# Thresholded attention on one core: GpSimd's queue held in the order of a written table, the second quad loaded by pairs, and another table

## The chip, the core and the metric

The kernel runs on one core of one Trainium2 chip. The metric is the device time of one execution in microseconds; lower is better. A core has five engines with a queue each: TensorE (PE in the profile, with its weight loads as PEld), VectorE (DVE), ScalarE (ACT), GpSimd (POOL) and SyncE (SP, which here only issues transfers). Transfers run on 16 DMA engines.

## The reference

Q, K and V are random float32 arrays of 8 batches, 12 heads, 512 positions and 64 dimensions; the threshold is 0.1.

```python
scores = einsum('bhqd,bhkd->bhqk', Q, K) * scale          # scale = 1/8
weights = exp(scores - max(scores)); weights /= sum(weights) + 1e-10
weights = where(weights > threshold, weights, 0)
weights /= sum(weights) + 1e-10
out = einsum('bhqk,bhkd->bhqd', weights, V)
```

On such data hardly a row has a weight above 0.1, so nearly the whole output is zero. The few rows that are not zero have one key each that passes.

## The kernel before, in words

The 96 heads are 48 pairs, the pairs are 24 quads (a quad is two pairs, four heads), and eight pairs are a group; there are six groups. The kernel does not compute the attention of every row. It writes zeros over the whole output, finds by rough tests the rows in which a weight may pass the threshold, and computes those rows exactly, at most 16 for each pair; a slow loop at the end takes over if there were more than that.

**For each quad**, the main part does these steps (names as in the table, function names with `do_` before them):

- `k`, `q` (lines 394 to 404, issued by SP): loads of K, four transfers of 128 KB, and of Q, one of 512 KB. K goes into a ring of four buffers, Q into one of three.
- `qcast` (GpSimd, line 411): Q to float16, one instruction for each pair.
- `ktr`, `qtr` (PE, lines 421 and 432): transposes of K and Q into PSUM.
- `kev`, `qev` (ACT or DVE, lines 387 and 389): copies of these from PSUM, two halves each.
- `kh` (GpSimd, line 391): the float32 keys to float16.
- `bits` (DVE, line 457) and `size` (PE, line 503): the norms of the rows, by a trick on the bits.
- `sc` (PE, line 467), `ex` (ACT, line 475, or DVE, line 477), `g` (PE, line 496): for each pair and each 128 keys the scores, their exponentials, and sums and sums of a high power over the keys, collected in one PSUM bank (`acc`) for the whole group. There are 384 exponentials of 128x512; ACT computes them by its table, DVE by shifting bits.
- `z` (SP, line 626): a write of 512 KB of zeros to the output.

**For each group**, a chain of small steps follows: `evac`, `test`, `flags`, `rank`, `key`, `oh`, `idx`, `idxev`, `base` find the rows to be computed; `gather` (GpSimd, line 556) fetches their Q by an indirect transfer, `split`, `xtr`, `xev`, `xqk`, `xexp`, `xcut`, `xkeep` compute their scores against all keys and find the key that passes; `xvi`, `xoi` make indices; `gv` (GpSimd, line 612) fetches the row of V by an indirect transfer, and `scatter` (GpSimd, line 619) writes it into the output by a third one. A scatter waits for its `gv` and for the zero writes of its group. The next group's sums wait for `evac`, since there is one `acc` bank.

**What sets the order.** All these steps are entered in a plan as numbered operations, and a long string, `ORDER`, lists them one by one: the number, the engine (A, D, G, P, S) and the buffers to take. `Plan.run` walks the string and traces each operation on the engine that it names. The framework then schedules what was traced by its own rules. To hold the written order, each instruction is wrapped in `keep`:

```python
keep = tc.keep_in_program_order
```

It ties an instruction to the instruction traced just before it on the same engine, and the framework may not swap those two. An indirect transfer is traced as two instructions on GpSimd, a register move (which the framework adds, without `keep`) and the transfer itself; `affine_select`, by which constants are made, has such a move too. No other operation of the table has one.

The string is found outside the kernel, by a search over a model of the engines. The numbers in it follow the order in which operations are entered: 12 constants first, then for each unit of loading its steps, after each fourth quad the 21 steps of its group, at the end five others. A unit is what is loaded and prepared together: a quad, but for quad 0, whose two pairs are two units.

Read out of the string, the order on SP and on GpSimd before is this (k, q, z and the casts with the number of their quad, a and b for its pairs where these are apart; gather, gv, split and scatter with their group):

```
SP:     k0a k0b q0b k1 q1 k2 q2 z0 k3 k4 q3 z1 z2 q4 k5 k6 q5 q6 z3 z4 q7 k7 q8 q9 z5 q10
        k8 k9 k10 k11 k12 q11 z6 z7 z8 z9 q12 k13 z10 k14 k15 q13 z11 q14 z12 q15 k16 q16 k17
        z13 q17 z14 q18 q19 k18 z15 q20 k19 z16 q21 k20 z17 q22 k21 q23 k22 z18 k23 z19 ... z23
GpSimd: tri test_a lane slot_no row_no key_i test_b qcast0a key_no test_w qcast0b kh0b
        qcast1 kh1 qcast2 kh2 kh3 qcast3 kh4 qcast4 kh5 qcast5 kh6 qcast6 gather0 qcast7 kh7
        split0 qcast8 qcast9 qcast10 gv0 kh8 kh9 scatter0 gather1 qcast11 kh10 split1 kh11
        qcast12 gv1 kh12 qcast13 kh13 scatter1 qcast14 kh14 qcast15 gather2 qcast16 kh15 split2
        qcast17 kh16 qcast18 gv2 kh17 qcast19 kh18 qcast20 scatter2 gather3 split3 qcast21 kh19
        qcast22 kh20 gv3 kh21 qcast23 kh22 scatter3 kh23 gather4 split4 gv4 gather5 split5
        scatter4 gv5 scatter5
```

(q0a is issued by ACT in both.)

Of the kernel before, what the change touches and what calls it, by code (L numbers as in the profile page):

```python
# [18 lines left out]
104S 114D 93A 97P1.6.12 96D 92A 87P 98D 99A 115P3.4.11 149P0.5 145S 95A 117D 118P1.6.10 150A6 100P 120D 151A
101P 119D 209S1 121P2.4.9 152G0 124P0.6.8 116D 123A 129P1.5.7 131A 122D 132P3.4.6 130A 127P 249S2 134D 126A  # L20
211P2.5 143D0 125A 135P1.4.5 148G0 212A5 213D 144P 128P 137A 136D 138P0.6.4 214G3 133A 153P2.5 140D 290S1 154A
141P 155D 139D 156P1.4.3 159P3.6.2 157A 162P2.5.1 158D 142P 161A 163D 165P0.1.0 164A 170P4.6.13 250S0 184D2 160A
210G1 173P2.5.12 171D 172A 185P 168P 175A 167D 291S2 176P3.4.11 174A 215P5.6 166D 177A 179P1.2.10 216D 169P 181A
217D 182P 180D 186S 252P0.3 178D 218P5.6.9 253D4 254A 221P1.2.8 183P 222A 248S 223D 255G2 224P3.4.7 220A 293P0.1
187D1 226A 227P2.6.6 219A 225D 332S1 188P4 229A 189D 230P 246D1 251G0 228A 190P 294A3 232P3.5.5 295D 235P2.6.4
331S0 233A 231P 234D 296G1 237A 247P 191D 256P0.1 236D 238P3.5.3 257A 241P4.6.2 292G1 192D1 244P 242A 243D 193P2
258A 394S0 239A 297P0.4 194D2 259P1.6.1 287D0 298A 196G1 261D 240A 288P 435S2 262P0.3.0 260A 195D 299D 245P 263A
264D 265P5.6.13 268P1.2.12 328D2 267A 273P0.4.11 333G0 271P 289S 275A 270D 329P 269A 276P3.6.10 266D 279P2.4.9
274A 277D 282P1.5.8 281A 476S1 272P 280D 283A 334P0.3 278A 284D 300P1.2.7 335A2 303P4.6.6 336D 393S3 285P 305A
301D 337G0 286P 302A 304D 306P0.5.5 309P3.6.4 307A 314P1.2.3 308D 197G1 312P 395G1 311A 316D 317P0.4.2 315A  # L30
434S2 320P5.6.1 318D 319A 198P2 321D 199A1 323P0.1.0 338P2.4 325A 324D 200P5 436G0 339A 322D 340A 310D 475S1
369D1 400P0.1 201A1 341P2.6.13 477G1 344P3.4.12 342D 313P 346A 326P 343D 345A 327P 202D 516S0 203D 370P 353P
347P2.5.11 205D 204D 396P3.4 349A 348D 206G2 397D1 398A 350P5.6.10 351A 352D 355P2.4.9 578S3 399G3 356A
358P3.5.8 357D 354P 360A 359D 361P2.6.7 364P4.5.6 363A 401D 367P 402D 362A 366D 437P0.3 517S0 365A 403P1.6.5
431D0 406P2.5.4 438A0 368P 407D 405A 330S 409P0.4.3 404A 372D0 412P2.6.2 410A 414D 373P1 413A 371S 432P 374D
411A 441P0.6 439D 375P 408A 417P2.4.1 376D 440G2 420P1.3.0 433S 418A 377D0 415P 422A 421D 416P 207G 419A 378P5
442A 443D 474S 423P2.3.13 379D1 426P1.4.12 380D 424D 425A 478P0.6 381G0 427A 429P 428D 579S2 479A9 444P3.5.11
472D2 518G0 447P1.2.10 480A 450P0.4.9 445D 448A 430P 473P 619S2 449A 446D 481G1 453P1.6.8 451A 452D 458P2.3.7
454A 456P 455D 459A 461P0.5.6 464P1.4.5 460D 463A 457P 466A 462D 467P2.6.4 515S 482P3.5 468A 469D 470P 483A 484D
519P0.4 465D 660S1 485P2.6.3 382G0 523P3.5 520D8 521A 383P1 471P 487A 486D 522G0 384A0 488P0.4.2 513D1 491P1.6.1  # L40
489A 385P2 580G1 493D 490A 701S0 492A 524D 525A 514P 554D0 497P 386A0 494P0.4.0 581P3.6 387D 496A 388D 620S1
499P1.5.13 582A7 555P 389D 502P2.4.12 500D 583A 391G1 495A 390D 505P3.6.11 556S 501D 504A 508P0.1.10 506D 584G3
503A 498P 510D 509A 526P4.5.9 529P2.3.8 661S0 528A 527D 511P 530A 532P0.1.7 507D 535P4.5.6 531A 533D 540P2.6.5
537A 618S 512P 542D 536A 538P 541A 534D 585P0.3 543P4.5.4 702S2 586A 587D 546P2.6.3 539P 545D 544A 621G0
549P1.3.2 616D2 547A 622P0.5 550A 551D 763S3 552P 548A 623D6 588P2.4.1 624A 591P1.3.0 553P 590D 589A 625G2
594P0.6.13 593D 592A 663P4.5 595A 557D1 597P1.2.12 392G 764S1 596A 602P0.3.11 664D5 665A 600P 662G1 617P 599A
603D 558P6 598A 605P4.5.10 804S2 559D 608P0.2.9 607A 606D 560P 666G1 601P 610A 561D 609D 604A 611P1.5.8 626P4.6
562D1 612A 667P0.2 703G0 614P 627A 628D 668D 659S 563P3 669A 657D1 613A 629P1.6.7 632P0.4.6 564D0 630D 631A 658P
# [784 lines left out]
```

## Time and profile before

| | |
|---|---|
| median of 3 runs | 193.63 us (192.74 to 194.64) |
| the profiled execution's own time | 194.19 us |
| its span, first to last instruction | 192.4 us |
| busy: PE, DVE, ACT, GpSimd | 170.1, 164.3, 146.7, 86.2 us |
| mean granted clock of PE | 0.955 |
| moved by DMA | 38.44 MB, 200 GB/s over the span |

In the rows of the profile an instruction stands as output<-input by tile names; L411 is line 411 of the kernel. A group's row ends with busy time, mean duration in ns, and the idle time of the engine ahead of these instructions with what ended it. The two rows of slices cut the span into 40 parts of 4.8 us; a digit is the busy share in tenths. In GpSimd's timeline the bracket holds the idle time before an instruction and the instruction that released it; a queue entry such as "POOLq MOVE" is one of the sequencer and not counted as busy.

### The profile page before, as it was taken

To read this page: it belongs to the slowest core of one execution; us is meant where nothing else is said; L and a number is where in the kernel's file an instruction comes from. 1 tells how busy PE (TensorE), PEld (TensorE's weight loads), DVE (VectorE), ACT (ScalarE), POOL (GpSimd) and SP (SyncE) were. 2 spreads that over 40 slices of the span, in tenths; PEclk is the share of its full clock that TensorE was granted. 3 is DMA by queue.
4 is the path that set the end of the run, shared out by engine and by line. 5 is a ranking of instruction groups with operands and counts; after the bars stand their busy time and mean duration, and the time that the engine had idled before them with its cause. 6 is when DMAs were issued, how large, how long until landed. Compare 5 with 4: busy or idle time off the path is not lost.

```text
span 192.4 us, 5896 instructions
## 1 busy us (share of the span) xinstructions
PE 170.1 (88%) x2272; PEld 69.7 (36%) x2272; DVE 164.3 (85%) x343; ACT 146.7 (76%) x295; POOL 86.2 (45%) x129
## 2 busy tenths in 40 slices
PE   7699969999998698999999999989999999997910
PEld 2343332443333143433453434433433533334300
DVE  7699978999999599999999999899799999996040
ACT  2679867799976588899999979979799898951010
POOL 7744243286552427255564534770442723103322
PEclk9889997999999889999999999999999999999975
DMA  5997898898988799989999996969895000000000
GB/s 135 257 269 213 200 376 191 253 363 203 347 173 189 169 354 345 227 200 319 300 266 326 282 291 197 282 184 235 226 382 202 1 3 0 10 0 5 8 2 8
DMA packets 67439, 38.44 MB, mean 200 GB/s; under 512 B 51882, under 2 KB 64240, under 8 KB 67408
## 3 DMA queue, kind: packets, MB, share of 16 engines
q1 hardware_dynamic: 66560, 37.50, 68.3%
q0 software_dynamic: 576, 0.27, 0.8%
q8 instruction: 19, 0.31, 0.7%
q10 hardware_dynamic: 272, 0.26, 0.5%
q14 instruction: 12, 0.10, 0.2%
HBM read 25.56 MB, written 12.78 MB: 199 GB/s over the span
## 4 chain that ended last, share of the span: by engine, by line
PE 40%; DVE 29%; DMA 11%; issue 9%; POOL 6%; SPq 2%; ACT 1%; POOLq 0%; DVEq 0%; ACTq 0%
DVE e L477 16%; PE bank L467 15%; PE acc L496 13%; DVE v L457 5%; DMA k<-in_K_dram 5%; PE bank L582 4%; PE bank L421 3%; DMA q<-in_Q_dram 3%; POOL qh L411 3%; DVE kt L389 2%; DMA vr<-in_V_dram,idx 2%; PE acc L503 2%; DVE qk L389 2%; PE bank L432 2%; POOL qk L391 2%
## 5 line engine op out<-in xcount | busy, mean ns | idle before, releaser
L475 ACT ACTIVATE e<-bank 128x512 f16<-128x512 f32 x226 | 118.5, 613 | 11.9 <-PE bank L467 11.0
L477 DVE TENSOR_SCALAR e<-bank 128x512 int16<-128x512 f32 x158 | 101.3, 682 | 4.7 <-PE bank L467 4.2
L467 PE MATMUL bank<-qk 64*128 64x512 f16 x384 | 67.6, 390 | 5.5 <-POOL qk L391 1.9
L496 PE MATMUL acc<-e,w_sum 128*32 128x512 f16 x384 | 57.7, 393 | 0.3 <-ACT e L475 0.2
L496 PE MATMUL acc<-e,w_pow 128*32 128x512 bf16 x384 | 57.4, 393 | 0.0
L411 POOL TENSOR_SCALAR qh<-q 128x512 f16<-128x512 f32 x48 | 34.1, 710 | 21.9 <-DMA q<-in_Q_dram 7.8
L391 POOL CAST qk<-kt 128x1024 f16<-128x1024 f32 (+1 forms) x24 | 24.8, 1036 | 27.0 <-ACT kt L387 12.4
L467 PEld LDWEIGHTS <-qk 64*128 64x128 f16 x384 | 18.3, 95 | 43.2 <-issue 35.8
L496 PEld LDWEIGHTS <-w_sum 128*32 128x32 f16 x384 | 13.9, 96 | 25.6 <-issue 20.0
L387 ACT COPY kt<-bank 128x512 f32<-128x512 f32 (+1 forms) x30 | 17.1, 588 | 7.6 <-PE bank L421 6.9
L457 DVE TENSOR_SCALAR v<-qk 128x1024 int32<-128x1024 int32 x24 | 19.0, 795 | 2.7 <-POOL qk L391 1.9
L421 PE MATMUL bank<-identity_f,k 64*128 64x64 f32 x384 | 17.5, 228 | 1.4 <-DMA k<-in_K_dram 1.3
L421 PEld LDWEIGHTS bank<-identity_f,k 64*128 64x128 f32 x384 | 15.5, 141 | 6.7 <-issue 2.6
L612 POOL DMA_INDIRECT vr<-in_V_dram,idx x6 | 6.5, 1084 | 22.1 <-DVE keys L528 9.7
L389 DVE COPY kt<-bank 128x512 f32<-128x512 f32 (+1 forms) x20 | 13.0, 659 | 1.5 <-PE bank L421 0.8
L496 PEld LDWEIGHTS <-w_pow 128*32 128x32 bf16 x384 | 13.6, 96 | 0.2
L619 POOL DMA_INDIRECT out_dram<-vr,idx x6 | 6.3, 1044 | 16.1 <-DVE e L477 4.7
L389 DVE COPY qk<-bank 128x512 f16<-128x512 f16 (+1 forms) x30 | 11.7, 411 | 1.8 <-PE bank L432 1.4
L387 ACT COPY qk<-bank 128x512 f16<-128x512 f16 (+1 forms) x20 | 10.9, 566 | 2.2 <-PE bank L432 2.2
L432 PE MATMUL bank<-identity_h,qh 64*128 64x64 f16 x384 | 10.5, 192 | 2.0 <-POOL qh L411 1.8
L432 PEld LDWEIGHTS <-qh 64*128 64x128 f16 x384 | 8.8, 96 | 9.1 <-POOL qh L411 4.6
L582 PE MATMUL bank<-kt,xq 128*32 128x512 f32 x96 | 11.6, 597 | 0.4 <-ACT xq L387 0.4
(95 smaller groups left out, 103.7 us busy)
## 6 DMA issues: line engine op xcount, KB each, us to landing
k<-in_K_dram SPq DMA_DIRECT2D x96, 128.0 KB
out_dram<-zero SPq DMA_DIRECT2D x24, 512.0 KB
q<-in_Q_dram SPq DMA_DIRECT2D x23, 512.0 KB
q<-in_Q_dram ACTq DMA_DIRECT2D x1, 256.0 KB
q<-in_Q_dram SPq DMA_DIRECT2D x1, 256.0 KB
qs<-in_Q_dram,idx POOLq DMA_INDIRECT x6, 4.4
vr<-in_V_dram,idx POOLq DMA_INDIRECT x6, 4.3
out_dram<-vr,idx POOLq DMA_INDIRECT x6, 2.5
```

The costliest lines, as they stand in the source:

```text
L387: keep(nc.scalar.copy(dst, src))
L389: keep(nc.vector.tensor_copy(dst, src))
L391: keep(nc.gpsimd.tensor_copy(dst, src))
L411: keep(nc.gpsimd.tensor_scalar(dst, src, ALPHA, 1.0, op0=ALU.mult, op1=ALU.mult))
L421: keep(nc.tensor.matmul(bank_at(("kp", u), i)[:, c:c + D], lhsT=src[ps, n0 + n, r, :], rhs=identity_f32[ps, ps], is_transpose=True, start= ...
L432: keep(nc.tensor.matmul(bank_at(("qp", u), i)[:].bitcast(f16)[:, c:c + D], lhsT=src[ps, n0 + n, r, :], rhs=identity_h[ps, ps], is_transpos ...
L457: keep(nc.vector.tensor_scalar(v_b[at("v", q)][:].rearrange("p a n c -> p (a n c)").bitcast(i32), qk_b[at("qk", q)][:].rearrange("p a n c ...
L467: keep(nc.tensor.matmul(bank_at(("sc", hp, t), h)[:], lhsT=qk[ps, 1, n, t * P:(t + 1) * P], rhs=qk[ps, 0, n, :], start=True, stop=True))
L475: keep(nc.scalar.activation(dst, src, ACTF.Exp, scale=math.log(2.0) / 1024.0, bias=exp_bias))
L477: keep(nc.vector.tensor_scalar(dst.bitcast(i16), src, EXP_BIAS * 1024.0, 0.0, op0=ALU.add, op1=ALU.max))
L496: keep(nc.tensor.matmul(acc[32 * j:32 * j + 32, :], lhsT=w, rhs=rhs, **turn(x, j)))
L582: keep(nc.tensor.matmul(bank_at(("xs", x))[32 * b:32 * b + 32, :], lhsT=xq[:, a * P + 32 * b:a * P + 32 * b + 32], rhs=kt_b[at("kt", GQ * ...
```

## The change

Three things change.

1. The walk over the table is put into the framework's `manual_schedule` for GpSimd. Inside it what is traced on GpSimd runs in the order in which it is traced, register moves included. The other engines have `keep` as before.
2. Quad 1, like quad 0, is loaded and prepared as two units of one pair. Its K transfers stay four of 128 KB; its Q becomes two of 256 KB; `ktr`, `kev`, `kh`, `qtr` and `qev` of this quad become twice as many with half the columns. The numbers from 102 on, behind this quad, shift by 10.
3. The string is another one, from a further search.

```diff
 ORDER = """
-12S3 13A2 5G 37S 2G 11D 0G 6G 38S 1D 64S2 7G 8G 10D 3G 15P0.1 14G1 16A9 18D3 19A 9G 20P2.3 17A 40P4.5 21A 65S1
-4G 22A 41D 23P0.6.13 42D 105S1 26P1.2.12 39G 25D 24A 29P3.4.11 28A 30D 43G 44P0.5 31A 32P2.6.10 27A 34D 33A 35P
...
+12S3 13A2 7G 8G 37S 5G 11D 38S 9G 64S2 6G 0G 88S 14G1 15P0.1 1D 18A3 2G 20P2.3 19A 21D 22A 10D 3G 40P4.5
+23P2.6.13 16D9 17A 4G 65S1 41D 42A 26P1.3.12 24A 25D 29P0.5.11 89S 39G 28A 32P2.4.10 27D 115S1 31A 43G 44P3.6
...
 """
...
-    units = [(0, 0, 1), (0, 1, 1)] + [(q, 0, 2) for q in range(1, NQ)]
+    units = [(q, n, 1) for q in range(2) for n in range(2)] + [(q, 0, 2) for q in range(2, NQ)]
...
-    plan.run(ORDER)
+    with tc.manual_schedule(engines={mybir.EngineType.Pool}):
+        plan.run(ORDER)
```

Read out of the new string in the same way:

```
SP:     k0a k0b q0b k1a k1b q1a q1b k2 q2 k3 q3 k4 z0 q4 k5 q5 k6 z1 z2 q6 z3 k7 q7 z4 z5 k8
        q8 k9 q9 z6 k10 z7 q10 k11 z8 q11 k12 z9 q12 q13 q14 k13 k14 k15 k16 k17 q15 z10 z11
        q16 q17 z12 z13 k18 k19 q18 q19 q20 z14 z15 k20 z16 q21 q22 q23 z17 k21 k22 z18 z19 k23
        z20 ... z23
GpSimd: row_no key_i tri key_no slot_no lane qcast0a test_a test_b test_w qcast0b kh0b kh1a
        qcast1a qcast1b kh1b qcast2 kh2 kh3 qcast3 kh4 qcast4 qcast5 kh5 kh6 qcast6 gather0
        qcast7 kh7 split0 qcast8 gv0 kh8 qcast9 kh9 scatter0 qcast10 kh10 gather1 qcast11 kh11
        split1 kh12 qcast12 qcast13 qcast14 gv1 kh13 kh14 scatter1 gather2 qcast15 split2 kh15
        kh16 qcast16 qcast17 gv2 kh17 qcast18 scatter2 qcast19 qcast20 kh18 gather3 kh19 qcast21
        kh20 split3 qcast22 kh21 gv3 qcast23 kh22 scatter3 kh23 gather4 split4 gv4 gather5
        split5 scatter4 gv5 scatter5
```

Counted by engine, the tables differ in this: exponentials on ACT 226 before and 236 after, on DVE 158 and 148; key copies `kev` on ACT 30 and 30, on DVE 20 and 22; query copies `qev` on ACT 20 and 20, on DVE 30 and 32; `kh` of pair 0a on ACT and DVE before, both halves on ACT after; `xev` on ACT 5 and 4 times, on DVE 1 and 2. From the last `evac` on, both strings have the same steps in the same order.

More of the change, by code (lines that the diff above doesn't have):

```diff
@@ L19 @@
[L19 to L48, printed above, removed]
@@ L79 @@
+1091P5.6.11 1119D0 1094P1.3.10 1075A 1076P 1092D 1093A 1120P 1097P2.4.9 1096A 1074D 1100P5.6.8 1099A 1098D
+1105P0.3.7 1121S 1102A 1077P 1095D 1107A 1108P2.4.6 1101D 1106A 1103P 1109A 1110D 1111P1.6.5 1114P3.5.4 1113A
+947G1 1104P 1112D 1115A 1117P 1116D 948P0 1118P 949A1 950P2 1122D0 1123P4 951A1 1124D 1125P 952D 953D 1143P 954D
+955D 1126D 956G1 1127D0 1146D 1128P6 1129D0 1144P 1130D 1131G0 1132G0 1133P1 1134A0 1135P3 1136A0 957G 1137D
+1138D 1139D 1147D 1141G0 1140D 1142G
 """
```

92 lines of the change are left out of this document (59 added, 33 removed).

## The prediction

> **What bounds the kernel now.** I read the page first (busy shares and the 40 slices), then the busy times by stretches that I cut where the slices dip, then GpSimd's own timeline, then the sources of the indirect transfers, and last the groups that price the added and removed operations.
>
> ```profile
> PE 170.1 (88%) x2272; PEld 69.7 (36%) x2272; DVE 164.3 (85%) x343; ACT 146.7 (76%) x295; POOL 86.2 (45%) x129
> PE   7699969999998698999999999989999999997910
> DVE  7699978999999599999999999899799999996040
> ```
>
> No engine is full over the whole span. PE looks fullest, but its matmuls overlap, so what can be packed is better read on DVE and ACT, which drain PSUM: every score tile needs one of them. Slices 5 and 13 of PE and DVE are holes, and the last slices are a tail. By stretches (columns: length, then PE, PEld, DVE, ACT, POOL busy with their counts, granted PE clock, DMA share, GB/s):
>
> ```profile
> 0.00:8.00 8.00, 5.21 (x37) 2.34 (x39) 5.06 (x36) 2.89 (x7) 6.20 (x34) 0.98 0.75 182
> 8.00:20.00 12.00, 11.65 (x162) 5.10 (x160) 11.20 (x21) 10.53 (x22) 5.72 (x8) 0.87 0.92 241
> 20.00:28.00 8.00, 6.14 (x92) 2.63 (x90) 6.64 (x11) 5.92 (x12) 2.28 (x3) 1.00 0.95 294
> 28.00:32.00 4.00, 3.97 (x34) 0.95 (x36) 2.92 (x5) 2.65 (x5) 2.18 (x3) 0.57 0.91 212
> 32.00:57.00 25.00, 24.14 (x361) 9.86 (x361) 24.27 (x45) 21.89 (x45) 13.90 (x18) 1.00 0.94 265
> 57.00:66.00 9.00, 6.59 (x92) 2.62 (x84) 6.71 (x15) 5.46 (x12) 3.49 (x4) 0.99 0.79 177
> 66.00:70.00 4.00, 4.00 (x48) 1.43 (x47) 3.32 (x7) 3.01 (x6) 0.21 (x1) 0.60 0.97 274
> 70.00:120.00 50.00, 48.67 (x710) 20.46 (x709) 48.08 (x92) 46.69 (x96) 25.43 (x31) 1.00 0.96 281
> 120.00:131.00 11.00, 10.07 (x155) 4.46 (x153) 10.35 (x22) 9.61 (x20) 7.59 (x8) 1.00 0.80 231
> 131.00:151.00 20.00, 19.40 (x265) 7.75 (x263) 18.38 (x36) 18.58 (x39) 7.03 (x9) 1.00 0.76 241
> 151.00:171.40 20.40, 19.58 (x282) 8.09 (x282) 20.40 (x39) 17.83 (x35) 6.58 (x8) 1.00 0.01 3
> 171.40:192.40 21.00, 10.64 (x80) 3.98 (x70) 6.95 (x26) 1.64 (x5) 5.53 (x6) 0.83 0.02 5
> ```
>
> I call length minus half of (DVE + ACT) the packing loss of a stretch. It is 4.0, 1.1, 1.7, 1.2, 1.9, 2.9, 0.8, 2.6, 1.0, 1.5 and 1.3 us for the eleven rows before the tail, 20.2 us of 171.4 in all. The quiet stretch 70 to 120 loses 2.6 of 50, 5.2%; that is my measure of a stretch without an accident. The tail of 21.0 us is a chain of small steps of the last group.
>
> The two holes have different causes, both visible on GpSimd (start, length, instruction, idle before it and what ended it):
>
> ```profile
> 26.65 1.32 POOL L411 TENSOR_SCALAR qh<-q 128x512 f16<-128x512 f32 x2 [3.44 <-DMA q<-in_Q_dram]
> 63.28 1.02 POOL L619 DMA_INDIRECT out_dram<-vr,idx  x1 [3.16 <-DMA vr<-in_V_dram,idx]
> 64.30 1.05 POOL L391 CAST qk<-kt 128x1024 f16<-128x1024 f32 x1
> 121.17 1.09 POOL L619 DMA_INDIRECT out_dram<-vr,idx  x1 [2.89 <-DVE qk L389]
> 150.01 1.02 POOL L619 DMA_INDIRECT out_dram<-vr,idx  x1 [4.72 <-DVE e L477]
> ```
>
> At 26.65 GpSimd waits for Q of quad 3. At 63.28 it stands 3.16 us before the scatter of group 0, whose rows from V are still in flight, and the key cast of quad 8 follows only at 64.30. In the table that scatter stands behind the key casts of quads 8 and 9. Group 2's scatter (121.17) runs ahead of four items that the table puts before it (key casts 17 and 18, query casts 19 and 20), and group 3's (150.01) ahead of three. So the queue that ran is not the table's. Why, the sources show:
>
> ```profile
> L612 POOLq MOVE  x6: 29/29/29, 56.1 to 179.8; - x6
> L619 POOLq MOVE  x6: 29/29/29, 58.8 to 184.9; - x6
> ```
>
> Each indirect transfer has a register move of 29 ns before it. The kernel's keep call ties an instruction to the one traced just before it on its engine, so the transfer is tied to its own move, and the move to nothing: the chain is cut there and what follows may slide ahead.
>
> Quad 8's late cast is what PE waits for next:
>
> ```profile
> 65.40 0.70 PE L467 MATMUL bank<-qk 64*128 64x512 f16 x4 [1.88 <-POOL qk L391]
> ```
>
> And the holes cost more than their idle time: after each, the granted clock falls (0.57 in 28 to 32, 0.60 in 66 to 70). [...]
>
> **The change, part by part.**
>
> 1. *Loads.* The new table queues SP as k2 q2 k3 q3 k4 z0 q4 k5 q5, the old one as k2 q2 z0 k3 k4 q3 z1 z2 q4 k5 k6 q5 (k, q: loads of a quad; z: 0.5 MB of zeros). Q of quad 3 now stands behind 0.5 MB of K and 0.5 MB of zeros fewer, at the 294 GB/s of the stretch 1.0 MB, some 3.4 us. It was in flight from 20.66:
>
> ```profile
> 20.66 5.81 DMA q<-in_Q_dram
> ```
>
> The wait of 3.44 us then goes. What 20 to 32 loses above 5.2% is 2.9 - 0.6 = 2.3 us; bounds 0 (the next quad's Q is late instead) to 2.9 (no loss at all). I take 2.3. Late next would be Q of quad 4, but it too moves forward: one zero write ahead of it and not three.
>
> 2. *GpSimd's queue, group 0.* The scatter goes behind the key casts of quads 8 and 9 (and now the query casts of 9). Quad 8's key copies were done at about 60.5 (59.78 and 0.69, below), so the cast can start there and not at 64.30, 3.8 us earlier. What 57 to 70 loses above 5.2% is 3.7 - 0.7 = 3.1 us. I take 2.5, since K of quad 8 itself landed late: its transposes were released by a load (56.05 to 58.8, below), which the new order of loads puts ahead of q8, q9 and q10. Bounds 0 to 3.7.
>
> ```profile
> 56.05 2.77 DMA k<-in_K_dram
> 59.78 0.69 DVE L389 COPY kt<-bank 128x512 f32<-128x512 f32 x1 [0.28 <-PE bank L421]
> ```
>
> The scatter itself costs GpSimd the same 1.0 us later, beside an engine 45% busy. What waits for it is only the free row buffer, of which there are three.
>
> 3. *Groups 1 to 3.* 120 to 131 loses 1.0, 0.5 above the quiet rate; 131 to 151 loses 1.5, 0.5 above. I take 0.6 of the 1.0; bounds 0 to 1.0. Group 1's scatter held a cast too, but it lies in the quiet stretch, so I count nothing there.
>
> 4. *Balance.* Ten exponentials move from DVE to ACT (158 to 148, 226 to 236, counted in the tables).
>
> ```profile
> L475 ACT ACTIVATE e<-bank 128x512 f16<-128x512 f32 x226 | 118.5, 613 | 11.9 <-PE bank L467 11.0 <-PE acc L496 0.2
> L477 DVE TENSOR_SCALAR e<-bank 128x512 int16<-128x512 f32 x158 | 101.3, 682 | 4.7 <-PE bank L467 4.2
> L387 ACT COPY kt<-bank 128x512 f32<-128x512 f32 x28 | 16.4, 603 | 4.2 <-PE bank L421 3.5 <-PE bank L467 0.6
> L387 ACT COPY kt<-bank 128x256 f32<-128x256 f32 x2 | 0.8, 382 | 3.4 <-PE bank L421 3.4
> L389 DVE COPY kt<-bank 128x256 f32<-128x256 f32 x2 | 0.8, 420 | 0.3 <-PE bank L421 0.3
> L389 DVE COPY kt<-bank 128x512 f32<-128x512 f32 x18 | 12.3, 685 | 1.2 <-PE bank L421 0.6 <-PE bank L467 0.5
> ```
>
> DVE loses 10 x 0.682 = 6.8, ACT gains 6.1. From 70 to 171.4 DVE was busy 97.2 us and ACT 92.7; levelling them can give half of the difference, 2.2. I take half of that, 1.1; bounds 0 to 2.2.
>
> 5. *Second quad by pairs.* Four key copies of 256 instead of two of 512 cost 2 x (0.382 + 0.420) - (0.603 + 0.685) = 0.3 us, the query copies by the same step about as much (an estimate), which shared by DVE and ACT is 0.3; SP issues one load more. Against it, 8 to 20 loses 1.1, of which 0.6 is the quiet rate, so at most 0.5 can come back. I take 0; bounds -0.3 to 0.5.
>
> 6. *Constants.* The nine sets of constants took GpSimd from 1.31 to 6.60 without the cast of 0.75 among them, and 0.61 later, 5.2 us. The new order puts six of the nine before the first query cast, by their share 3.4 us (an estimate; bounds 3.4 and 5.2), so it starts at about 4.7 and not at 3.87. PE transposes the first keys before it needs that cast, from 5.47:
>
> ```profile
> 1.31 0.15 POOL L288 MEMSET limits<- 128x64 f32 x1
> 3.87 0.75 POOL L411 TENSOR_SCALAR qh<-q 128x512 f16<-128x512 f32 x1
> 6.38 0.22 POOL L279 CAST test_w<-test_f 128x48 bf16<-128x48 f32 x1
> 8.03 0.61 POOL L325 CAST key_no<-key_i 128x512 f32<-128x512 int32 x1
> 5.47 0.46 PE L421 MATMUL bank<-identity_f,k 64*128 64x64 f32 x8 [0.60 <-DMA k<-in_K_dram]
> ```
>
> The cast ends at about 5.5, just covered; each further microsecond would come at full price. Zero, bounds 0 to 1.6 lost (the cast ending at 7.1).
>
> 7. *Tail.* Both tables have the last group's steps in the same order on every engine. In the queue that ran, the scatter of group 4 went ahead of the last split, but the split waited for its rows anyway (0.17 us). Zero.
>
> ```profile
> 179.82 0.40 POOL L563 TENSOR_TENSOR qb<-qs,ix 128x128 f32<-128x128 f32 x1 [0.17 <-DMA qs<-in_Q_dram,idx]
> ```
>
> 8. *Shorter leads.* I count the exponentials between a Q load and its cast in the tables. Quads 7 to 12 had 15, 24, 29, 20, 17, 19 and get 13, 10, 11, 15, 15, 14; quad 18 goes from 28 to 12. With 384 exponentials in about 163 us, ten are 4.3 us, less than the 5.81 us above. SP runs ahead of the table where a buffer is free, so not each is late; I charge 0.9 us, bounds 0 to the rival below.
>
> Sum: 2.3 + 2.5 + 0.6 + 1.1 - 0.9 = 5.6 us. The profiled execution took 194.19 (its span of 192.4 and 1.8 around it), so 188.6; it lies 0.56 above the median of 193.63, so the forecast for the median is **188.0 us**. With all terms at their good ends, 2.9 + 3.7 + 1.0 + 2.2 + 0.5 = 10.3, it is 183.3.
>
> **The rivals.**
>
> *Starved for Q (slower).* GpSimd's queue is now strict, so a query cast that waits for its load holds key casts and gathers behind it. Place: quads 7 to 12, 15 and 18. Price: what 20 to 32 paid for one such wait, 2.3 us. The gains before term 8 are 6.5, so it decides from the third late quad on; five give 193.63 - 6.5 + 11.5 = 198.6. For it: DMA share of 0.94 and 0.96 in 32 to 57 and 70 to 120. Against: in 120 to 151 it is 0.80 or less, and K waits less behind Q. 12%.
>
> *Only GpSimd's part lasts (no change).* The loads stay the limit of the first 60 us, with the same bytes, and balance gives nothing: 193.63 - 2.5 + 0.9 = 192.0. For it: the DMA shares above. Against: 0.5 MB zero writes have slack until the scatter of their group and are what is moved. 18%.
>
> *Port contention.*
>
> ```profile
> L457 DVE TENSOR_SCALAR v<-qk x24: 675/694/1328, 10.8 to 165.8; 128x1024 int32<-128x1024 int32 x24
> L411 POOL TENSOR_SCALAR qh<-q x48: 615/620/1152, 3.9 to 152.9; 128x512 f16<-128x512 f32 x48
> ```
>
> Some of DVE's SBUF to SBUF passes take twice their median, and so do some query casts. If every one of the 24 met a cast at 1.33 instead of their mean of 0.795, DVE would lose 12.8 us, half of it on the end: 188.0 + 6.4 = 194.4. [...] Nothing says that the new order makes them meet more often. 5%.
>
> *Not what it says.* If transfers still slide, terms 2 and 3 return: 188.0 + 3.1 = 191.1. For it: an order per engine must bind moves too. 4%.
>
> **How the numbers follow.** The forecast has 61%. A measurement here tells about 1% (1.9 us) from no change. Faster (below 191.7): nearly all of the forecast, the last rival and a third of the second, 0.68. Within 1%: the rest of the second, most of the port case and a little of the forecast, 0.18. Slower: 0.14, mostly starvation. The range goes from the good ends, 183.5, to 194.5, which takes in all but starvation; the forecast's own range is 185 to 191.5.
>
> **What would show it.** Each indirect transfer's move directly before it in GpSimd's queue, and the order of the table; the key cast of quad 8 before the scatter, no idle of 1.9 us on PE behind it, clock 1.00 from 57 to 70; GpSimd's wait for Q of quad 3 below 1 us and the main part ending near 166; ACT near 153 us busy, DVE near 158; a tail of 21. Wrong would be waits of GpSimd for Q at quads 7 to 12 over 2 us each, or the last exponentials still at 170.

## The result and the profile after

| | before | after |
|---|---|---|
| median | 193.87 us (4 runs, 192.74 to 194.64) | 187.13 us (4 runs, 185.75 to 188.53) |
| ratio | | 0.9657, 95% interval 0.9569 to 0.9745 |
| the profiled execution and its span | 194.19 and 192.4 us | 186.93 and 185.2 us |
| mean granted clock of PE | 0.955 | 0.986 |

In a later series the changed kernel took 184.89 us, ratio 0.962 (0.9548 to 0.9693), profiled span 183.0. So the ratio of one kernel differed by 0.4% between two series, and its span by 2.2 us between two profiled executions; smaller differences between series are not read below. Medians here and below are of all runs of a kernel, while ratios and intervals leave out the slow runs, those more than 1.5% above the kernel's fastest: six of the ten of "old table held", and the profiled one of "scatter 0 early".

The page of the changed kernel, the same rows as of before and the row of the granted clock:

```profile
PE 167.5 (90%) x2272; PEld 69.0 (37%) x2272; DVE 157.2 (85%) x337; ACT 148.8 (80%) x305; POOL 85.7 (46%) x130
PE   7896999999999999999999998999999999998700
DVE  6897899999979979879898999999999999955040
PEclk9999999999999999999999999999999999999995
```

The hole of PE in slice 13 is gone, and the granted clock stays full from the start to the tail (1.00 in every stretch below up to 163.60 us). A dip is left in slice 3, where GpSimd waits 4.34 us, until 17.89, for Q of quad 2. By stretches, cut as before up to 151 us (same columns; 32 to 57 is left out, see below):

```profile
0.00:8.00 8.00, 6.30 (x41) 2.73 (x41) 5.54 (x37) 3.36 (x8) 6.68 (x35) 1.00 0.69 175
8.00:20.00 12.00, 10.49 (x162) 4.50 (x161) 10.82 (x22) 9.96 (x23) 5.10 (x8) 1.00 0.88 224
20.00:28.00 8.00, 7.88 (x118) 3.39 (x110) 7.22 (x14) 7.75 (x17) 3.15 (x4) 1.00 1.10 270
28.00:32.00 4.00, 4.00 (x72) 1.91 (x74) 3.59 (x7) 4.00 (x9) 2.47 (x4) 1.00 1.11 259
57.00:66.00 9.00, 8.54 (x126) 3.55 (x127) 8.88 (x17) 8.91 (x19) 5.23 (x7) 1.00 1.15 304
66.00:70.00 4.00, 3.99 (x64) 1.77 (x60) 3.06 (x8) 4.00 (x10) 2.91 (x4) 1.00 1.09 272
70.00:120.00 50.00, 48.88 (x698) 20.18 (x698) 46.37 (x89) 45.69 (x94) 25.61 (x32) 1.00 0.92 264
120.00:131.00 11.00, 10.93 (x172) 4.46 (x163) 11.00 (x22) 10.38 (x21) 6.60 (x8) 1.00 1.00 279
131.00:151.00 20.00, 19.76 (x281) 7.74 (x279) 19.81 (x39) 18.37 (x39) 7.45 (x10) 1.00 0.61 200
151.00:163.60 12.60, 12.27 (x161) 4.61 (x161) 11.55 (x24) 11.68 (x24) 2.79 (x3) 1.00 0.02 4
163.60:185.20 21.60, 10.60 (x78) 3.91 (x70) 6.19 (x24) 1.64 (x5) 5.53 (x6) 0.88 0.03 6
```

The packing loss (length less half of DVE + ACT) is 0.7 us from 20 to 32, where it was 2.9, and 0.6 from 57 to 70, where it was 3.7. From 70 to the tail it is 4.0 + 0.3 + 0.9 + 1.0 = 6.2, where it was 2.6 + 1.0 + 1.5 + 1.3 = 6.4. The first 20 us lose 5.2 (5.1 before), and from 32 to 57, with DVE and ACT busy 23.20 and 23.01 of 25 us, 1.9 (1.9 before). The tail is 21.6 and not 21.0. GpSimd at the two places:

```profile
23.29 1.31 POOL L412 TENSOR_SCALAR qh<-q 128x512 f16<-128x512 f32 x2
53.11 1.73 POOL L412 TENSOR_SCALAR qh<-q 128x512 f16<-128x512 f32 x2 [4.53 <-DMA q<-in_Q_dram]
55.12 1.11 POOL L613 DMA_INDIRECT vr<-in_V_dram,idx  x1 [0.28 <-issue]
56.23 1.05 POOL L392 CAST qk<-kt 128x1024 f16<-128x1024 f32 x1
...
60.76 1.04 POOL L392 CAST qk<-kt 128x1024 f16<-128x1024 f32 x1 [2.08 <-ACT kt L388]
61.95 1.10 POOL L620 DMA_INDIRECT out_dram<-vr,idx  x1 [0.16 <-issue]
```

The query cast of quad 3 (23.29) no longer waits. The queue from 53 to 62 is the table's: query cast 8, fetch of group 0's rows, key cast 8, query cast 9, key cast 9, scatter 0. The scatter now finds its rows there.

A second reading serves for all kernels below: the start of the 113th, 145th and last of the 384 exponentials, counted in each trace, and the span (us; in brackets the differences). "Held" is with `manual_schedule` on GpSimd, "floating" without; the kernels are described with their experiments.

| kernel | 113th | 145th | last | span |
|---|---|---|---|---|
| before | 56.2 | 74.2 (18.0) | 170.1 (95.9) | 192.4 (22.3) |
| after | 51.3 | 66.6 (15.3) | 162.3 (95.7) | 185.2 (22.9) |
| after, later series | 50.3 | 65.5 (15.2) | 160.1 (94.6) | 183.0 (22.9) |
| new table floating | 51.1 | 72.2 (21.1) | 167.3 (95.1) | 190.2 (22.9) |
| scatter 0 early | 50.6 | 73.4 (22.8) | 168.1 (94.7) | 191.1 (23.0) |
| floating, gap filled | 51.0 | 71.3 (20.3) | 166.8 (95.5) | 190.0 (23.2) |
| old table held | 54.7 | 69.6 (14.9) | 164.7 (95.1) | 187.1 (22.4) |
| new table, old loads | 55.5 | 70.6 (15.1) | 165.3 (94.7) | 188.3 (23.0) |
| old table held, new loads | 54.3 | 69.2 (14.9) | 164.7 (95.5) | 187.0 (22.3) |
| the same, balance | 54.1 | 69.4 (15.3) | 164.7 (95.3) | 187.2 (22.5) |
| scatters 1 to 3 early | 50.5 | 65.7 (15.2) | 160.7 (95.0) | 183.4 (22.7) |
| Q1 in one transfer | 50.5 | 65.7 (15.2) | 160.3 (94.6) | 183.2 (22.9) |
| tail order | 51.0 | 66.3 (15.3) | 161.0 (94.7) | 182.4 (21.4) |
| three pieces | 50.1 | 65.3 (15.2) | 160.9 (95.6) | 182.0 (21.1) |

Three places change: up to the 113th (the loads), from there to the 145th (scatter 0), and the tail. The exponentials behind the 145th take 94.6 to 95.9 us in every kernel. The two profiles of the changed kernel differ by 1.0 us at the 113th, so a smaller difference there is not read as one. Each row is one execution, and that of the kernel before is a long one: 194.19 us, where its medians in the later series are 192.61 to 193.47.

### The profile page after: what moved, and what is told of

It reads as the page before. It is cut to its first block, busy times and chain, and to the rows that moved or that the text cites. A ratio compares the mean times of both kernels' runs of the same rounds, so it can differ in the third digit from the quotient of the medians.

```text
span 185.2 us, 5894 instructions
## 1 busy us (share of the span) xinstructions
PE 167.5 (90%) x2272; PEld 69.0 (37%) x2272; DVE 157.2 (85%) x337; ACT 148.8 (80%) x305; POOL 85.7 (46%) x130
## 4 chain that ended last, share of the span: by engine, by line
PE 51%; DVE 15%; ACT 11%; issue 8%; DMA 6%; SPq 5%; POOL 1%; POOLq 0%; ACTq 0%; DVEq 0%
PE bank L468 17%; PE acc L497 16%; ACT e L476 10%; DVE e L478 6%; PE bank L583 5%; PE bank L422 5%; SPq L399 4%; DMA k<-in_K_dram 3%; PE bank L433 3%; PE acc L504 2%; DVE v L458 2%; DVE kt L390 2%; DVE oh L533 2%; PE bank L543 1%; DMA vr<-in_V_dram,idx 1%
## 5 line engine op out<-in xcount | busy, mean ns | idle before, releaser
L476 ACT ACTIVATE e<-bank 128x512 f16<-128x512 f32 x236 | 122.0, 631 | 7.6 <-PE bank L468 6.4
L478 DVE TENSOR_SCALAR e<-bank 128x512 int16<-128x512 f32 x148 | 93.6, 680 | 1.6 <-PE bank L468 1.4
L468 PE MATMUL bank<-qk 64*128 64x512 f16 x384 | 66.3, 380 | 2.6 <-DVE e L478 0.5
L497 PE MATMUL acc<-e,w_sum 128*32 128x512 f16 x384 | 56.8, 383 | 0.1
L392 POOL CAST qk<-kt 128x1024 f16<-128x1024 f32 (+1 forms) x25 | 25.8, 1034 | 40.5 <-DVE kt L390 24.3
L412 POOL TENSOR_SCALAR qh<-q 128x512 f16<-128x512 f32 x48 | 32.5, 678 | 20.0 <-DMA q<-in_Q_dram 10.2
L497 PEld LDWEIGHTS <-w_sum 128*32 128x32 f16 x384 | 13.8, 95 | 25.7 <-issue 20.6
L458 DVE TENSOR_SCALAR v<-qk 128x1024 int32<-128x1024 int32 x24 | 17.1, 720 | 0.7 <-ACT qk L388 0.6
L388 ACT COPY kt<-bank 128x512 f32<-128x512 f32 (+1 forms) x30 | 15.8, 567 | 0.8 <-PE bank L422 0.3
L390 DVE COPY kt<-bank 128x512 f32<-128x512 f32 (+1 forms) x22 | 14.1, 659 | 2.3 <-PE bank L422 2.1
L583 PE MATMUL bank<-kt,xq 128*32 128x512 f32 x96 | 11.5, 598 | 0.4 <-ACT xq L388 0.4
L201 PE MATMUL acc<-idle 128*128 128x512 f16 x32 | 9.3, 449 | 1.2 <-DVE idle L197 1.2
```

The source lines that it names most:

```text
L388: keep(nc.scalar.copy(dst, src))
L390: keep(nc.vector.tensor_copy(dst, src))
L392: keep(nc.gpsimd.tensor_copy(dst, src))
L412: keep(nc.gpsimd.tensor_scalar(dst, src, ALPHA, 1.0, op0=ALU.mult, op1=ALU.mult))
L458: keep(nc.vector.tensor_scalar(v_b[at("v", q)][:].rearrange("p a n c -> p (a n c)").bitcast(i32), qk_b[at("qk", q)][:].rearrange("p a n c ...
L468: keep(nc.tensor.matmul(bank_at(("sc", hp, t), h)[:], lhsT=qk[ps, 1, n, t * P:(t + 1) * P], rhs=qk[ps, 0, n, :], start=True, stop=True))
```

## The experiments

My theory after the result: the hold is worth its money at scatter 0, the earlier loads give the rest, and balance and the other scatters give next to nothing. The rival: the new table is simply the better one, and the hold or the loads alone do little.

### What the hold is worth in the new table

```diff
-    with tc.manual_schedule(engines={mybir.EngineType.Pool}):
-        plan.run(ORDER)
+    plan.run(ORDER)
```

> The changed kernel without the held queue: the new table and units, but the register moves float again, so each scatter runs right behind its V gather, ahead of two or three casts. My theory (hold, loads and balance each carry a part; hold 3.1 us): about 190.2, 189 to 191.5, with a wait of GpSimd of 2 to 4 us before most scatters. Rival 'the table alone does it': 187.1, within 1 us of the changed kernel. Rival 'the held queue does it all': 192.5 or more.

191.91 us (10 runs) against 193.04, ratio 0.9958 (0.9906 to 1.0009): without the hold the new table is hardly better than the old kernel, so the rival falls. In GpSimd's timeline the scatter of group 0 stands ahead of key cast 8 again; those of groups 2 and 3 slide too:

```profile
61.50 1.01 POOL L620 DMA_INDIRECT out_dram<-vr,idx  x1 [5.60 <-DMA k<-in_K_dram]
121.35 1.02 POOL L620 DMA_INDIRECT out_dram<-vr,idx  x1 [7.32 <-PE bank L468]
153.32 1.10 POOL L620 DMA_INDIRECT out_dram<-vr,idx  x1 [3.95 <-issue]
```

The two late ones cost nothing: the 145th to the last exponential take 95.1 us. To see that it is the place of scatter 0 and nothing else that floats, one move was made with the queue held:

```diff
-GpSimd: ... gv0 kh8 qcast9 kh9 scatter0 qcast10 ...
+GpSimd: ... gv0 scatter0 kh8 qcast9 kh9 qcast10 ...
```

> The changed kernel with one move in its table: the scatter of group 0 stands right behind the transfer that fetches its rows, ahead of the key casts of quads 8 and 9; everything is still held. If the scatter's place is what the hold is worth, this one move costs nearly what the whole queue without the hold cost: GpSimd stands some 5 us before the scatter, the 128th exponential starts at 63 to 65 us and not at 59.8, the span is about 189.5, and the ratio to the kernel before is about 0.99 (the changed kernel 0.966). If instead the other indirect transfers that slid ahead made the loss (the gathers, which hold no key cast for rows in flight), the 128th exponential stays at 60 and the ratio at 0.966.

191.28 us (10 runs) against 192.61, ratio 0.9913 (0.9864 to 0.9962); the changed kernel in the same series 184.89, 0.962. One transfer three steps too early costs 6.4 us, as much as leaving out the whole hold (by the ratios 0.9913 and 0.9958, against 0.962 and 0.9657 of the changed kernel). The expectation named the wrong exponential: the 128th still starts at 58.3, and the gap opens just behind it, with the 129th at 65.3. GpSimd, and what PE waits for behind it:

```profile
54.30 1.11 POOL L613 DMA_INDIRECT vr<-in_V_dram,idx  x1 [3.47 <-DMA out_dram<-zero]
62.14 1.02 POOL L620 DMA_INDIRECT out_dram<-vr,idx  x1 [6.73 <-DMA k<-in_K_dram]
63.16 1.04 POOL L392 CAST qk<-kt 128x1024 f16<-128x1024 f32 x1
```

```profile
64.26 1.03 PE L468 MATMUL bank<-qk 64*128 64x512 f16 x4 [5.61 <-POOL qk L392]
```

In its stretches DVE and ACT nearly stop (1.42 and 2.94 of 5 us, then 1.36 and 0.64 of 4), and the clock falls:

```profile
57.00:62.00 5.00, 1.65 (x28) 0.69 (x24) 1.42 (x3) 2.94 (x7) 0.00 (x0) 1.00 1.05 282
62.00:66.00 4.00, 1.74 (x12) 0.27 (x12) 1.36 (x3) 0.64 (x2) 3.69 (x4) 0.68 1.07 282
```

The bracket at 62.14 names a load of K that landed last in the profile; the entry of GpSimd's queue that belongs to the scatter waits until the fetched rows have landed, at 61.33. How long such a fetch is in flight, from the DMA issues within the few us around it, first before, then the changed kernel in its later series, then this one (last column: us from issue to landing):

```profile
vr<-in_V_dram,idx POOLq DMA_INDIRECT x1, 4.0
```

```profile
vr<-in_V_dram,idx POOLq DMA_INDIRECT x1, 5.3
```

```profile
vr<-in_V_dram,idx POOLq DMA_INDIRECT x1, 7.0
```

With the new table the transfers are denser at this place (DMA share 1.15 from 57 to 66 in the changed kernel, 0.79 before), the fetch takes longer and a scatter right behind it holds GpSimd longer. This fetch takes 4.0 to 4.7 us in the four traces with the old table and 5.3 to 7.2 in the ten with the new one, wherever the scatter stands. The cost follows GpSimd's wait before the scatter: 3.16 us of wait in the kernel before and 3.1 us lost between the 113th and the 145th exponential, 5.60 and 5.8 with the new table floating, 6.73 and 7.5 with scatter 0 early. So the hold is worth more in the new table than in the old. In the changed kernel the row of the queue (packets, MB, share of the 16 engines), which holds the 18 indirect transfers, some 15 KB each, and the times to landing of its six fetches of V are:

```profile
q0 software_dynamic: 576, 0.27, 0.7%
```

```profile
DMA to landing us min/median/max: 2.4/4.0/7.2
```

The quickest takes 2.4 us; the one that matters here takes two to three times as long (5.3 to 7.2 with the new table), among other transfers.

### What the hold is worth in the old table

```diff
-    plan.run(ORDER)
+    with tc.manual_schedule(engines={mybir.EngineType.Pool}):
+        plan.run(ORDER)
```

(on the kernel before)

> The kernel before with only the held queue: old table and units. My theory: 193.9 - 3.1 = 190.8 (189.5 to 192), the key cast of quad 8 before the scatter of group 0 and no half clock after 65 us; the half clock from 28 to 32 stays, since Q of quad 3 is still late. Rival 'the table alone does it': 193.9, within 1 us of the kernel before. Rival 'the held queue does it all': 187 to 188.

190.3 us (10 runs), ratio 0.9804 (0.9742 to 0.9867). From the 113th to the 145th exponential it takes 14.9 us and not 18.0: the 3.1 us of scatter 0. 1.5 us more lie ahead of the 113th. What of that is the hold (constants with register moves stand there too) and what is a difference between executions, these runs do not separate. One expectation missed: the half clock from 28 to 32 us is gone as well (granted 1.00 from 20 to 57), though GpSimd still waits 2.22 us for Q of quad 3.

### The loads

```diff
-SP: ... k1a k1b q1a q1b k2 q2 k3 q3 k4 z0 q4 k5 q5 k6 z1 z2 q6 z3 k7 q7 ...
+SP: ... k1a k1b q1a q1b k2 q2 z0 k3 k4 q3 z1 z2 q4 k5 k6 q5 q6 z3 k7 q7 ...
```

(the new table, held, with the old table's order of the first loads)

> The changed kernel with the old order of SP's early loads (z0 before K of quad 3, Q of quad 3 behind K of quad 4, z1 and z2 before Q of quad 4); from quad 8 on SP is unchanged. My theory (term 1 is 2.3 us): 189.4 (188.4 to 190.5), with a GpSimd wait of 2 us or more for Q of quad 3 and a half clock near 28 us. Rival 'early loads are made good later, since the ring limits the loads anyway': 187.1, within 0.7.

190.47 us (9 runs), ratio 0.9919 (0.9865 to 0.9973). The 113th exponential starts at 55.5 and not at 51.3 or 50.3 (the two profiles of the changed kernel); behind it nothing changes. GpSimd waits 2.89 us for Q of quad 3, as expected, and 5.19 for that of quad 2; the half clock comes at 20.6 to 24.0 us (0.79 on the mean from 20 to 28) and not near 28. So in the new table the order of the loads is worth 4 to 5 us. The opposite edit, on the kernel before with the hold:

```diff
-SP: ... k1 q1 k2 q2 z0 k3 k4 q3 z1 z2 q4 k5 k6 q5 q6 ...
+SP: ... k1 q1 k2 q2 k3 q3 k4 z0 q4 k5 q5 k6 z1 z2 q6 ...
```

> The kernel before with the held queue and the new order of SP's early loads (Q of quad 3 ahead of K of quad 4, zero writes 0 to 2 later), nothing else of the new table. My theory now: the hold was worth 2.7 us on the old table and the loads 4.1 in the changed kernel, so 193.0 - 2.7 - 4 = 186.3 (185 to 188), about the changed kernel's time, with a tail of 20.2 from the last evacuation on and not 21.6. Rival 'the rest of the new table (balance, pairs) is needed to keep the early loads' gain': 189 to 190.5.

188.7 us (4 runs) against 193.47, ratio 0.9759 (0.9625 to 0.9893), not to be told from the hold alone; by the traces the 113th exponential gains 0.4 us, less than two executions of one kernel differ by. My theory of 186.3 falls, and the rival (189 to 190.5) is nearer. Q of quad 3 did come earlier, first with the old loads, then with the new:

```profile
25.79 1.32 POOL L411 TENSOR_SCALAR qh<-q 128x512 f16<-128x512 f32 x2 [2.22 <-DMA q<-in_Q_dram]
```

```profile
23.58 1.32 POOL L411 TENSOR_SCALAR qh<-q 128x512 f16<-128x512 f32 x2
```

The old table makes little use of it. A first explanation was that DVE is its next limit. From 20 to 57 us, one row each for the old table held, the same with the new loads, and the changed kernel in its later series:

```profile
20.00:57.00 37.00, 35.16 (x515) 14.36 (x516) 36.02 (x65) 31.45 (x64) 17.95 (x23) 1.00 0.94 270
```

```profile
20.00:57.00 37.00, 35.26 (x525) 14.81 (x519) 36.17 (x67) 31.38 (x64) 17.72 (x23) 1.00 0.98 274
```

```profile
20.00:57.00 37.00, 35.79 (x521) 15.19 (x517) 34.44 (x66) 34.81 (x71) 18.07 (x23) 1.00 1.00 282
```

DVE is busy 36.2 of 37 us in the old table while ACT has 5.6 to spare; the new table has them level. If that was the reason, moving a few exponentials should free it:

```diff
-DVE: ex 17, 35, 48, 64, 112 (in the order of the table)
+ACT: ex 17, 35, 48, 64, 112
```

(on the kernel of the last experiment)

> The kernel before, held, with the earlier loads (187.0 us of span, 0.9759, its 113th exponential at 54.3 us, VectorE busy 36.2 of the 37 us from 20 to 57 and ScalarE 31.4), and five of the first 112 exponentials moved from VectorE to ScalarE, as many as the other table has there, one and two apart at most: the second of two in a row on VectorE each time. If the earlier loads brought nothing there because VectorE was the next limit, the five free 5 x 0.68 = 3.4 us of it, ScalarE has room for their 3.1 us, the 113th exponential starts at 51 to 52.5 us, the span is 184 to 185.5 and the ratio about 0.962. If it is not VectorE but the order of the key work in the old table that cannot use the earlier Q, the 113th exponential stays at 54 us, the span at 187, and the ratio at 0.976.

189.1 us (6 runs) against 193.47, ratio 0.9801 (0.975 to 0.9853), the 113th exponential at 54.1. The row moved as planned and the time did not:

```profile
20.00:57.00 37.00, 35.44 (x529) 14.98 (x524) 34.09 (x63) 33.34 (x68) 17.80 (x24) 1.00 1.00 281
```

So the explanation by DVE falls. What DVE gave up it then spent waiting. Where the two tables part can be read from the traces. The 33rd exponential starts at 20.67 us in this kernel and at 21.03 in the later profile of the changed kernel, the 113th at 54.08 and 50.27. Between the two, first this kernel, then the changed one:

```profile
20.67:54.08 33.41, 31.85 (x463) 12.94 (x459) 30.65 (x54) 31.13 (x63) 16.66 (x22) 1.00 1.01 289
```

```profile
21.03:50.27 29.24, 28.25 (x417) 12.13 (x417) 28.32 (x53) 28.53 (x58) 13.69 (x17) 1.00 1.01 287
```

Of the 4.2 us of difference 1.7 are packing loss (2.5 against 0.8). The rest is work: DVE and ACT do 61.8 us against 56.9 for the same 80 exponentials, and part of that the new table had done by the 33rd already (32.6 us against 30.4). By this reading it is the old table's order of the other work on DVE and ACT, with the standing that goes with it, that makes little use of the loads; which of its steps, these runs do not show.

### The clock

```diff
         qk = qk_b[at("qk", q)]
+        if hp == 16 and t == 0:
+            for _ in range(16):
+                keep(nc.tensor.matmul(bank_at(("sc", hp, t), 0)[:], lhsT=idle[:, 0:P], rhs=idle[:], start=True, stop=True))
         for h in range(2):
```

(on the new table floating: filler matmuls in PE's wait for key cast 8)

> The new table with the floating queue, and 16 filler matmuls of 128x512 on PE right before the first scores of quad 8, into the bank which these scores then overwrite; so PE works through 3.4 us of the hole at 60 to 64. My theory that the hole costs more than its idle time through the clock: no half clock after the hole and about 1 us less than the floating queue's 191.9 (190.4 to 191.4). Rival 'the clock costs nothing, since DVE and ACT set the pace behind the hole': 191.9, within 0.4, at a full clock. Third: the fillers delay the scores, 192.5 or more.

189.75 us (5 runs) against 193.47, ratio 0.9825 (0.973 to 0.9921). Floating without fillers, then with them (the third column from the end is the granted clock):

```profile
62.00:66.00 4.00, 2.38 (x30) 0.71 (x31) 2.01 (x4) 1.08 (x2) 3.75 (x5) 0.50 1.01 295
66.00:70.00 4.00, 4.00 (x44) 1.03 (x39) 3.43 (x7) 2.74 (x6) 1.81 (x3) 0.70 1.20 308
```

```profile
62.00:66.00 4.00, 2.32 (x33) 0.73 (x33) 2.20 (x4) 1.08 (x2) 3.75 (x5) 1.00 1.00 298
66.00:70.00 4.00, 3.92 (x50) 1.40 (x46) 3.96 (x9) 3.70 (x8) 2.02 (x3) 1.00 1.19 310
```

The clock stays full, and DVE and ACT do 7.7 us of work from 66 to 70 and not 6.2. Half of the difference is 0.75 us, and 0.8 is what the 113th to the 145th exponential gain (20.3 against 21.1). By the ratios it is 1.3%, 2.6 us, with intervals that overlap a little, and the profiled execution with fillers is the slowest of its five (191.73). So of the 6 to 7 us that scatter 0 costs, the lost clock may be 1 to 2.5, an estimate from these two readings, and the standing engines the rest.

### Pieces that change nothing, and the tail

```diff
-GpSimd: ... gv1 kh13 kh14 scatter1 ... gv2 kh17 qcast18 scatter2 ... gv3 qcast23 kh22 scatter3 ...
+GpSimd: ... gv1 scatter1 kh13 kh14 ... gv2 scatter2 kh17 qcast18 ... gv3 scatter3 qcast23 kh22 ...
```

(on the changed kernel)

> The changed kernel, queue held, but with the scatters of groups 1, 2 and 3 written into the table right behind their V gathers, where the floating queue has them; the scatter of group 0 stays. My theory now: only group 0's place costs time, so no change, ratio 0.965 (within 0.5%), although GpSimd waits 3 to 7 us before each of the three. Rival (my prediction's term 3): 0.6 us or more slower, and nearer to the 191.9 of the floating queue if every early scatter costs.

184.89 us (4 runs) against 193.47, ratio 0.9588 (0.9483 to 0.9692). GpSimd waits 3.01, 7.81 and 5.13 us before the three, and nothing is lost: their places are worth nothing.

```diff
         q, n0, k = u
+        if q == 1:
+            if n0:
+                return
+            k = 2
```

(in the changed kernel's loads of Q: quad 1 in one transfer of 512 KB)

> The changed kernel with Q of quad 1 loaded by one transfer of 512 KB; the steps of quad 1 stay split by pairs. My theory (term 5 is zero): 187.1, within 0.7. Rival 'the early arrival of the first pair is what the split brings': 188 to 188.5, with the first query cast of quad 1 a microsecond later than 11.2.

185.26 us (4 runs) against 193.04, ratio 0.9696 (0.9624 to 0.9768). Two transfers for quad 1's Q instead of one are worth nothing either. That its steps are split by pairs was not taken back.

The tail had grown, from 20.2 us between the start of the last evacuation (L506 before, 172.20) and the end, to 21.6. In the changed kernel:

```profile
163.37 1.91 PE L583 MATMUL bank<-kt,xq 128*32 128x512 f32 x16
163.60 0.81 DVE L507 TENSOR_SCALAR ev<-acc,root_of 128x512 int32<-128x512 int32 x1 [0.66 <-PE acc L497]
165.21 0.34 PE L513 MATMUL bank<-test_w,ev 128*128 128x48 bf16 x4
```

The exact scores of group 4 (L583) stand in PE's queue right ahead of the test of group 5, which could have started at 164.41 and starts 0.80 us later. They have time; the test begins the last chain. So I moved group 4's exact part behind the gather of group 5:

```diff
-PE: ... xqk4 test5 rank5 ... spare(acc, 17) ...
+PE: ... test5 rank5 ... base5 xqk4 ... spare(acc, 8) ...
```

(the other engines' steps of both groups in the same order; `spare` are filler matmuls on an idle tile, which stand on PE behind the index's matmuls)

> The changed kernel with the tail's order changed: the last group's steps up to its gather before the exact scores of group 4 on PE, their key step on DVE and their V gather on GpSimd; 8 filler matmuls instead of 17. My theory: the tail of 21.6 us is 1.3 longer than before's, since the test waits 0.80 us behind the exact scores of group 4 and the gather 0.5; DVE's key step of group 4 (about 1.2 us) leaves the path too. So 1.5 to 2.5 us less than the changed kernel, ratio 0.954 to 0.959 of before. Rival 'the chain of the last group is bound by its transfers, and group 4 then ends last': no change, ratio 0.965.

183.75 us (4 runs, 183.51 to 184.13) against 193.47, ratio 0.9521 (0.943 to 0.9612), the tail 20.0 us:

```profile
162.38 0.81 DVE L507 TENSOR_SCALAR ev<-acc,root_of 128x512 int32<-128x512 int32 x1 [0.72 <-PE acc L497]
163.24 0.34 PE L513 MATMUL bank<-test_w,ev 128*128 128x48 bf16 x4 [0.92 <-DVE ev L507]
```

From the start of the last evacuation to the index that the last gather needs (`idx`) it takes 4.9 us before, 5.6 in the changed kernel and 4.1 here; from the gather to the end 15.0, 15.2 and 15.2. So the gain lies ahead of the gather, in the test and in DVE's key step of group 4, and the fewer fillers, which come behind, have no part in it.

The last three edits together, and the changed kernel beside them:

> The changed kernel with three edits that each read 0.4 to 1.4% lower than it alone: the tail's order, one transfer for quad 1's Q, and scatters 1 to 3 right behind their fetches. If the three gains are separate, the median is 193.5 less 9.3 (the tail's order), less 1 for each of the two others, about 182, ratio 0.942. If the two others only read low by chance (neither removes a wait from the path that the trace shows), it is as the tail's order alone, 183.8, ratio 0.952.

183.78 us (4 runs, 183.44 to 184.38) against 192.61, ratio 0.9562 (0.9491 to 0.9632): as the tail's order alone.

> The changed kernel itself, beside the two others on one chip: ratio 0.966, span 185, if the ratios of different calls may be put beside each other within half a per cent; otherwise only those of one call may.

184.89 us (4 runs, 184.43 to 185.58). So the three pieces together are worth 1.1 us (183.78 against 184.89). The tail's order alone, beside the changed kernel with scatters 1 to 3 early in its own series, is worth as much (183.75 against 184.89), and 1.5 by the tails in the traces (20.0 against 21.5). The two other edits add nothing.

## Why the prediction was right, and where its steps were off

The forecast of 188.0 us holds (187.13), though the gain was under-sized: 5.6 us forecast, 6.7 measured and 7.7 in the later series (192.61 to 184.89). By the measure of packing loss the profiled execution gained 2.2 us from 20 to 32, 3.1 from 57 to 70 and 0.2 from 70 to the tail, and lost 0.6 in the tail as it was cut there. DVE and ACT together were busy 4.2 us less ahead of the tail, half of which is 2.1. That is 7.0 of the 7.2 us of span. The main part ended at 163.6 and not near 166.

1. *Loads, 2.3.* The wait for Q of quad 3 went, and the loss from 20 to 32 fell by 2.2. But the step treated the term as one that can be added by itself. It can't: the new loads gain 4 to 5 us in the new table and some 0.4 in the old. Of the bounds 0 to 2.9 the lower one is about true for the old table, and the upper one is too low for the new.
2. *Scatter 0, 2.5.* The mechanism was right; the term was under-sized. It is 3.1 in the old table, and in the new one, where the fetch takes longer, 6.4 by the times and 5.8 to 7.5 by the traces. "Not what it says" was put at 191.1; the two kernels with scatter 0 early took 191.91 and 191.28.
3. *Groups 1 to 3, 0.6.* Nothing (0.2 by packing loss, none with the scatters early): the waits of GpSimd at 121 and 153 us, seen with the new table floating, have cover.
4. *Balance, 1.1.* DVE came out at 157.2 us as forecast (158), ACT at 148.8 and not at 153:

```profile
L476 ACT ACTIVATE e<-bank 128x512 f16<-128x512 f32 x236 | 122.0, 631 | 7.6 <-PE bank L468 6.4
L478 DVE TENSOR_SCALAR e<-bank 128x512 int16<-128x512 f32 x148 | 93.6, 680 | 1.6 <-PE bank L468 1.4
```

   I had multiplied counts by means. Exponentials overlap on their engine: 226 of 613 ns are 138.5 us, and the row said 118.5 busy. Ten more cost ACT 3.5 us of busy time, not 6.1, and ten fewer took 7.7 off DVE's row (101.3 to 93.6). Their net of 4.2 is as much as the whole fall of busy time above, so by the measure of packing loss the move could be worth 2.1 us, near the upper bound. Whether it saved any time is not shown: five moved in the old table gave nothing, the exponentials behind the 145th take what they took, to within the 1 us by which executions differ, and the new table without the move was not run.
5. and 6. *Quad 1 by pairs, constants, 0.* Nothing speaks against it: quad 1's Q in one transfer changes nothing, the first query cast started at 4.9 us, where 4.7 was worked out, and the first 20 us lose 5.2 us after and 5.1 before.
7. *Tail, 0.* Wrong by 1.4 us, measured from the last evacuation. I compared the tables from the last evacuation on, where they agree. The difference stands just ahead of it: the new table puts group 4's exact scores on PE between the last sums and the test. I had read the order of the steps within the tail and not what each of its engines still had in its queue when it began.
8. *Shorter leads, -0.9.* Of quads 7 to 12 only quad 8 waited over 2 us for its Q (4.53 us at 53.11), and PE was busy 5.00 of 5 us from 48 to 53: no hole came of it. DVE and ACT were busy 7.62 and 7.63 of 9 us from 48 to 57, a loss of 1.4, 0.9 above the quiet rate; that this is the price of the wait is not shown. The starved rival (198.6) needed five such waits with a hole each; there was none. The port case (194.4) did not come: DVE's pass over the bits takes 720 ns on the mean, and took 795. Before, eight of its 24 passes took over 700 ns (784 to 1328), and each of the eight began while GpSimd was in a cast or, once, in a split (L563); after, three did (882, 1006 and 1066), each begun during a cast. That a port is the cause no run shows.

```profile
L458 DVE TENSOR_SCALAR v<-qk 128x1024 int32<-128x1024 int32 x24 | 17.1, 720 | 0.7 <-ACT qk L388 0.6
```

"Only GpSimd's part lasts" (192.0) would have been right for the hold in the old table in kind (the loads give nothing there), but not for this change. So terms that were too high and terms that were too low met: the tail and the scatters 1 to 3 against scatter 0 and the loads, with balance open. That the sum came out within 1 us is luck in that part. The single effects do not add up either: taking back the hold costs some 6 us and taking back the loads 4 to 5, more than the gain of the whole change; the new table without both was not run. Two small slips bear on nothing: the good ends add up to 183.3, while the range was given from 183.5, and ten exponentials of 384 in 163 us are 4.2 us and not 4.3.

## What to carry to other kernels

In these traces an instruction that waited for a transfer just issued stopped all that was queued behind it on GpSimd (3.16 to 6.73 us ahead of scatter 0). Its price was then not its own microsecond but up to about the transfer's time in flight at that place, among the other transfers (4.0 to 7.2 us): 3 to 7.5 us where the next key cast stood behind it, nothing at the scatters 1 to 3, where what stood behind had time. A better order of loads was worth only what the rest of the order could use (4 to 5 us in one table, some 0.4 in the other), so price it by swapping it both ways: into the new order and out of it. Ahead of a last chain of small steps, look at what each engine still has in its queue; work of an earlier stage that has time belongs behind the first step of the chain.

## What the runs showed of the hardware

How long PE ran at half clock: 3.4 us after the hole of 1.88 us before (65.8 to 69.2); with scatter 0 early 6.8 us, from 63.4, 0.9 us ahead of the end of the 5.61 us hole, to 70.3. What sets these lengths the runs do not show. One stretch at half clock cost next to nothing: the old table held with new loads ran at half from 9.2 to 12.6 us and the same with balance did not, yet their 33rd exponentials start at 20.9 and 20.7.

In these traces an indirect transfer that carries its own wait starts sooner than one behind a separate wait in GpSimd's queue. The gather of group 5 needs the index that `idxev` writes (the bracket names the step behind it, but the gather of group 2 before starts at 101.70 us, while that step ends at 102.10). Before, it started 0.27 us after its index was done (177.07); in the changed kernel, where one wait entry of 17 ns for the index stands ahead of it, 0.77 us after (169.23):

```profile
176.85 0.22 DVE L546 TENSOR_SCALAR idx<-bank,slot_add 128x1 int32<-128x1 f32 x1 [0.17 <-PE bank L542]
...
177.34 1.00 POOL L556 DMA_INDIRECT qs<-in_Q_dram,idx  x1 [0.92 <-DVE ix L551]
```

```profile
169.01 0.22 DVE L547 TENSOR_SCALAR idx<-bank,slot_add 128x1 int32<-128x1 f32 x1 [0.18 <-PE bank L543]
...
170.00 1.00 POOL L557 DMA_INDIRECT qs<-in_Q_dram,idx  x1 [1.42 <-DVE ix L552]
```

It is 0.27 in all four traces with the old table and 0.77 or 0.78 in all ten with the new one. The scatter of group 0 shows the same: before it carried its wait and started 0.27 us after its rows had landed (63.01), with scatter 0 early it stood behind a separate entry and started 0.81 us after (61.33). That is 0.5 us of the longer tail, beside the 0.8 us of the late test. With the tail's order it is there still (the gather at 167.23, 0.78 after its index), and the gain ahead of the index makes good for it. It was read in the traces and not tried by itself.
